# Two of four weight sums made by an accumulating transfer, in a decoder layer on one Trainium2 core

## The chip, the cores and the metric

The kernel runs on one core of a Trainium2 chip. A core has five engines with a queue each, which run side by side and wait for one another through semaphores: TensorE (PE, matrix products; its weight loads are listed as PEld), VectorE (DVE), ScalarE (ACT), GpSimd (POOL) and SyncE (SP). Transfers between the memory and the core's own store (SBUF) are issued from an engine's queue and carried out by 16 DMA engines. Matrix products go to PSUM, a small store from which ScalarE and VectorE fetch them. The metric is the device time of one execution in microseconds (us); less is better.

## The reference

One decoder layer on 512 tokens of width 1024, all in float32: a SwiGLU feed-forward (hidden width 2816), a mixing part with dilated attention (12 heads of 128) beside a gated recurrence, and a second feed-forward, each with a norm before and after. Cut to what matters here:

```python
def swiglu(x, w_gate, w_up, w_down):
    return (jax.nn.silu(x @ w_gate) * (x @ w_up)) @ w_down

f = swiglu(rms_norm(h, ffn1_norm_pre[l]), ffn1_w_gate[l], ffn1_w_up[l], ffn1_w_down[l])
h = h + 0.5 * rms_norm(f, ffn1_norm_post[l])
u = rms_norm(h, mix_norm_pre[l])
proj = u @ w_in[l]                       # q, k, v, xr, yr and the branch gates
...
f = swiglu(rms_norm(h, ffn2_norm_pre[l]), ffn2_w_gate[l], ffn2_w_up[l], ffn2_w_down[l])
h = h + 0.5 * rms_norm(f, ffn2_norm_post[l])
```

The weights that this case is about are blocks of 128 columns of the up and gate matrices of both feed-forwards, and pairs of such blocks of `w_in` (a query block with a key block, and pairs of branch-gate blocks).

## The kernel before

**Split products.** TensorE works with a reduced float format (float32r). Each float32 operand is split in a high and a low part: ScalarE copies the value into the reduced format (L302) and VectorE subtracts that from the value (L303). A product then takes three matmuls: high by high, high by low, low by high.

**Seven products for eight.** Two column blocks of 128 (u and g) times the activations are a two-by-two block product: each weight block has two halves along the contracted dimension (u0, u1, g0, g1, each 128 x 512 as stored), and the activations are halved along the contracted dimension and along the tokens. A scheme of the Strassen kind makes it with seven products, p1 to p7, of half-size operands. It needs sums of weight blocks: u0+u1, u0+g0, u0+u1+g0 and u0+u1+g0+g1. A pair of blocks that is treated so is called a pair below. There are 16 in the first feed-forward (hidden blocks 6 to 21), 12 for queries and keys and 4 for branch gates in the attention stage, and 19 in the second feed-forward (blocks 3 to 21): 51.

**`w_forms`** prepares a pair. It loads the block u = (u0, u1) and the block g = (g0, g1), 512 KB each, into two tiles `raw` (tag raw, four buffers, filled through SyncE's queue), makes the four sums on VectorE (L691, L692, L693, L696; the first two go to a tile `s12` of tag `s`, two buffers), and splits all into four tiles: a (g0 for p1, g1 for p2), b (the tile s12, for p6 and p5), c (u after its first half was overwritten, for p7 and p4), and d (for p3). a, b and c come from the four buffers of tag w8, d from the two of tag w4. The products run in the order p1, p5, p6, p2, p7, p3, p4 (`seven_on`, `seven_wide`), only in the feed-forward blocks below 5 in the order p1, p2, p6, p5, p7, p4, p3 (`seven`). Their results are moved and summed out of PSUM by ScalarE and VectorE (L743, L792, L800, L950, L955).

**Order.** Tags are pools of buffers: a tile waits until an earlier holder of its buffer has been read for the last time. The order of the instructions in each engine's queue is laid out beforehand by a planner that takes the ready instruction of highest priority by its own estimate of durations and landings; `high_priority` moves the weight work ahead by AHEAD = 100 places and the fetching of results from PSUM by EVAC = 200. The pair for block f+1 is prepared in front of the products of block f. At run time each queue is worked in order, and an instruction that waits holds up all behind it.

**Around it.** In the feed-forwards the down product runs in between, four steps for each part of four hidden blocks, with forms of its own in the w8 buffers (`d_forms`, L986 to L1000). The tag `s` in the same pools also holds two sums of the activations (`forms_of`, tiles ts, or `x_forms`) until these are split, before the first pairs of a stage. GpSimd's queue issues other transfers: residual rows (h, kept), gains (L449), copies of activation forms (L655) and a rearrangement of values (L1239). The recurrence stage prepares its pairs with another function, `w_forms_within`, which uses no tile of tag `s`.

Of the kernel before, what the change touches and what calls it, by code (L numbers as in the profile page):

```python
# [10 lines left out]
F32 = mybir.dt.float32  # L11
F32R = mybir.dt.float32r
AF = mybir.ActivationFunctionType
ALU = mybir.AluOpType
AX = mybir.AxisListType

P = 128
T = 512
D = 1024
KC = D // P  # L20
NF = 22
FF_PARTS = ((0, 4), (4, 8), (8, 12), (12, 16), (16, 22))
NSTD = {1: 6, 2: 3}

SEVEN = range(4)
STEPS_AT = {1: ((6, 7, 7, 8), range(9, 13), range(13, 17), range(17, 21)),
# [5 lines left out]
RAW_W = 1024  # L32
# [3 lines left out]
AHEAD = 100  # L36
# [29 lines left out]
def ffn_order(n):  # L66

    order = [("std", f) for f in range(NSTD[n])]  # L70
    after = {}
# [3 lines left out]
    ready = False  # L75
    for f in range(NSTD[n], NF):
        if not ready:
# [106 lines left out]
def hybrid_layer(ctx: ExitStack, tc: tile.TileContext, xT: bass.AP, xN: bass.AP, wst: bass.AP,  # L184
                 first: bass.AP, rows: bass.AP, consts: bass.AP, bias: bass.AP, out: bass.AP):
    nc = tc.nc
    DVE, ACT, PE = nc.vector, nc.scalar, nc.tensor
# [3 lines left out]
    wpool = ctx.enter_context(tc.tile_pool(name="wpool", bufs=4))  # L191
# [39 lines left out]
    groups = stream_groups()  # L231
    state = {"g": 0, "i": 0, "off": 0, "raw": None, "ahead": AHEAD, "split": None}
# [68 lines left out]
    def split(dh, dl, src):  # L301
        state["split"] = ACT.activation(dh, src, AF.Copy).ins  # L302
        state["low"] = DVE.tensor_sub(dl, src, dh.bitcast(F32)).ins  # L303
# [377 lines left out]

    spool = [None]

    def w_forms(key):

        with tc.high_priority(offset=AHEAD):
            ur, gr = raw_two(key)
            u0, u1, g0, g1 = (r[:, i * 512:(i + 1) * 512] for r in (ur, gr) for i in range(2))
            s12 = spool[0].tile([P, 2, 512], F32, name="s12", tag="s", bufs=2)
            s1, s2 = s12[:, 0, :], s12[:, 1, :]  # L690
            DVE.tensor_add(s2, u0, u1)  # L691
            DVE.tensor_add(s1, s2, g0)  # L692
            DVE.tensor_add(u0, u0, g0)  # L693
            a, b, c, d = w8(), w8(), w8(), w4()
            split(a[:, 0, :], a[:, 1, :], gr)
            DVE.tensor_add(g1, s1, g1)  # L696
            split(b[:, 0, :], b[:, 1, :], s12.rearrange("p s c -> p (s c)"))
            split(c[:, 0, :], c[:, 1, :], ur)
            split(d[:, 0, :], d[:, 1, :], g1)
            lo, hi = slice(0, 512), slice(512, 1024)  # L700
            return {"p1": a[:, :, lo], "p2": a[:, :, hi], "p6": b[:, :, lo], "p5": b[:, :, hi],
                    "p7": c[:, :, lo], "p4": c[:, :, hi], "p3": d}
# [156 lines left out]
    def ffn(n, x, r, forms_x, apool, pss):  # L859
# [206 lines left out]

        keys = [(w, n, i) for i in range(NSTD[n]) for w in ("gate", "up")]
        forms = {}
        for ev in ffn_order(n):
            if ev[0] == "std":  # L1070
                j = ev[1]
                while len(pss) < 2 * j + 2:
                    pss.append(acc_ps())
                    gemm(pss[-1], fetch(keys[len(pss) - 1]), x)
                with tc.high_priority(offset=EVAC if j == NSTD[n] - 1 else 0):
                    std_out(pss[2 * j], pss[2 * j + 1], j)

                for step in steps[j:] if j == min(NSTD[n], 4) - 1 else steps[j:j + 1]:
                    step()
# [44 lines left out]
    for k in range(KC):  # L1124
        wh, wl, raw = wts[k]
# [77 lines left out]
    with ExitStack() as mx:  # L1203
# [291 lines left out]
        for c in range(0, KC, 2):  # L1495
            g, u = tmp("g"), tmp("u")
# [12 lines left out]
    with ExitStack() as mx:  # L1509
# [183 lines left out]
        for c in range(KC):  # L1693
            if c < 3:
                ps = pss[c]
            else:
# [25 lines left out]
    grow5, _ = gains(ap2, 4)  # L1722
# [138 lines left out]
```

## Time and profile before

| what | value |
|---|---|
| runs | 1209.45, 1208.63, 1209.24 us, median 1209.24 |
| profiled execution | 1209.61 us, its span 1207.8 us |
| busy PE / DVE / ACT / POOL | 1198.6 / 1033.3 / 831.8 / 26.1 us |
| first feed-forward's pairs | about 72 to 310 us from the span's start |
| pairs of attention | about 407 to 665 us |
| second feed-forward's pairs | about 898 to 1150 us |
| moved by DMA | 149.77 MB |

The span runs from the first to the last instruction. In the lists, "L303 DVE TENSOR_TENSOR w<-s,w" is line 303 of the kernel on VectorE, writing a tile w from tiles s and w; "x51 | 62.2, 1220 | 3.2 <-ACT w L302" are count, busy us, mean ns of one, and the us that the engine stood idle in front of them, with what ended that. Rows in order of time have start, duration, engine, line, operation and tiles. The rows of waits have the engine and line that waited, what for, the us in total, how often and the longest. Rows of stretches have, for each engine, the busy us and the number of instructions, then the granted clock, the DMA engines' busy share and GB/s.

### The profile page before, as it was taken

The page shows a single profiled execution, that of the slowest core. Times are in us where ns is not written, and L with a number is a line of the kernel's source. Part 1 is how long each engine was busy: PE and PEld are TensorE (multiplying, and loading weights), DVE is VectorE, ACT ScalarE, POOL GpSimd, SP SyncE. Part 2 cuts the span into 40 slices and gives each one's busy share as a digit, 9 for nine tenths or more (in the row PEclk, how much of TensorE's full clock was granted, in tenths as well). Part 3 has the DMA queues.
Part 4 walks back from the last instruction along what each step waited for, and adds up shares of the span by engine and source line. Part 5 has one row for each costly group of instructions (what it writes and reads, how often), then busy time and mean ns, then how long its engine had stood idle before and what let it go on. Part 6 is the DMA issues. An engine that isn't in the chain of part 4 may idle for free.

```text
span 1207.8 us, 18850 instructions
## 1 busy us (share of the span) xinstructions
PE 1198.6 (99%) x7222; PEld 1070.1 (89%) x7222; DVE 1033.3 (86%) x1626; ACT 831.8 (69%) x1447; POOL 26.1 (2%) x51
## 2 busy tenths in 40 slices
PE   9999999999999999999999999999999999999997
PEld 8889999999888888888888888888899999999996
DVE  7999888989689899999868999774799888889964
ACT  6566787887566576777736988734566687778763
POOL 0000000000011000000000000000100000000000
PEclk9999999999999999999999999999999999999999
DMA  7224343434725232222323532235443333333441
GB/s 267 88 92 139 120 139 109 137 117 150 250 106 154 71 101 91 89 87 80 122 67 110 176 121 88 88 107 189 140 142 121 121 125 117 128 120 126 125 173 70
DMA packets 45819, 149.77 MB, mean 124 GB/s; under 512 B 5152, under 2 KB 8608, under 8 KB 45728
## 3 DMA queue, kind: packets, MB, share of 16 engines
q1 hardware_dynamic: 38160, 131.09, 32.9%
q0 software_dynamic: 7280, 17.30, 4.3%
q8 instruction: 56, 0.92, 0.3%
q14 instruction: 35, 0.29, 0.1%
q10 hardware_dynamic: 288, 0.17, 0.0%
HBM read 138.06 MB, written 6.29 MB: 120 GB/s over the span
## 4 chain that ended last, share of the span: by engine, by line
PE 92%; DVE 4%; DMA 2%; ACT 1%; issue 1%; DVEq 0%; ACTq 0%
PE acc L779 10%; PE acc L729 9%; PE acc L731 9%; PE acc L730 9%; PE acc L315 7%; PE acc L317 7%; PE acc L316 7%; PE acc L780 5%; PE aux L1043 4%; PE aux L1044 4%; PE aux L1045 4%; PE acc L433 2%; PE acc L432 2%; PE acc L431 2%; DVE w L303 2%; DMA raw<-in_w 2%
## 5 line engine op out<-in xcount | busy, mean ns | idle before, releaser
L303 DVE TENSOR_TENSOR w<-raw,w 128x1024 fp32r<-128x1024 f32 (+1 forms) x272 | 296.9, 1097 | 32.2 <-ACT w L302 31.4
L302 ACT ACTIVATE w<-raw 128x1024 fp32r<-128x1024 f32 (+1 forms) x272 | 259.5, 958 | 90.0 <-PE acc L317 48.2
L729 PE MATMUL acc<-big,w 128*128 128x256 f32 x860 | 243.6, 283 | 0.0
L731 PE MATMUL acc<-big,w 128*128 128x256 f32 x860 | 243.4, 283 | 0.0
L730 PE MATMUL acc<-big,w 128*128 128x256 f32 x860 | 243.3, 283 | 0.0
L729 PEld LDWEIGHTS acc<-big,w 128*128 128x128 f32 x860 | 164.8, 192 | 1.8
L730 PEld LDWEIGHTS acc<-big,w 128*128 128x128 f32 x860 | 164.8, 192 | 1.5
L731 PEld LDWEIGHTS acc<-big,w 128*128 128x128 f32 x860 | 164.8, 192 | 0.0
L779 PE MATMUL acc<-big,w 128*128 128x512 f32 x380 | 136.5, 398 | 0.0
L780 PE MATMUL acc<-big,w 128*128 128x256 f32 x380 | 107.5, 283 | 0.0
L1043 PE MATMUL aux<-w,xf 128*128 128x512 f32 x224 | 87.3, 392 | 0.6 <-ACT w L302 0.6
L1044 PE MATMUL aux<-w,xf 128*128 128x512 f32 x224 | 87.5, 391 | 0.0
L1045 PE MATMUL aux<-w,xf 128*128 128x512 f32 x224 | 87.2, 389 | 0.0
L779 PEld LDWEIGHTS acc<-big,w 128*128 128x128 f32 x380 | 71.4, 188 | 16.0 <-ACT acc L784 0.2
L780 PEld LDWEIGHTS acc<-big,w 128*128 128x128 f32 x380 | 71.7, 189 | 0.3
L303 DVE TENSOR_TENSOR w<-s,w 128x1024 fp32r<-128x1024 f32 x51 | 62.2, 1220 | 3.2 <-ACT w L302 2.7
L315 PE MATMUL acc<-xf,w 128*128 128x512 f32 (+1 forms) x168 | 59.2, 354 | 0.0
L316 PE MATMUL acc<-xf,w 128*128 128x512 f32 (+1 forms) x168 | 58.7, 350 | 0.0
L317 PE MATMUL acc<-xf,w 128*128 128x512 f32 (+1 forms) x168 | 58.5, 349 | 0.0
L302 ACT ACTIVATE w<-s 128x1024 fp32r<-128x1024 f32 x51 | 53.9, 1057 | 6.2 <-PE acc L731 3.0
L779 PE MATMUL acc<-rb,w 128*128 128x512 f32 x152 | 55.5, 397 | 0.0
L743 ACT ACTIVATE c<-acc 128x256 f32<-128x256 f32 x68 | 25.8, 383 | 35.3 <-PE acc L731 35.3
(458 smaller groups left out, 2919.5 us busy)
## 6 DMA issues: line engine op xcount, KB each, us to landing
raw<-in_w SPq DMA_DIRECT2D x232, 512.0 KB, 3.5
big<-xf POOLq DMA_DIRECT2D x6, 512.0 KB, 3.3
gains<-in_rows POOLq DMA_DIRECT2D x5, 512.0 KB, 5.4
h<-in_x SPq DMA_DIRECT2D x8, 256.0 KB, 5.1
h<-in_xn POOLq DMA_DIRECT2D x4, 512.0 KB, 6.7
kept_m<-h POOLq DMA_DIRECT2D x4, 512.0 KB, 2.9
vals<-in_w SPq DMA_DIRECT2D x4, 512.0 KB, 6.0
h<-kept_m POOLq DMA_DIRECT2D x4, 512.0 KB, 6.2
```

Source lines behind the costliest of these rows:

```text
L302: state["split"] = ACT.activation(dh, src, AF.Copy).ins
L303: state["low"] = DVE.tensor_sub(dl, src, dh.bitcast(F32)).ins
L315: PE.matmul(ps, wh, xh, start=first, stop=False)
L316: PE.matmul(ps, wh, xl, start=False, stop=False)
L317: PE.matmul(ps, wl, xh, start=False, stop=last)
L729: PE.matmul(ps, wh, xh, start=start and k == 0, stop=False, skip_group_check=True)
L730: PE.matmul(ps, wh, xl, start=False, stop=False, skip_group_check=True)
L731: PE.matmul(ps, wl, xh, start=False, stop=k == 3, skip_group_check=True)
L779: PE.matmul(part, wh, at(BOTH, k), start=start and k == 0, stop=False, skip_group_check=True)
L780: PE.matmul(cross, wl, at(0, k), start=False, stop=k == 3, skip_group_check=True)
L1043: PE.matmul(ps, xh, wh, start=first and j == 0, stop=False, skip_group_check=True)
L1044: PE.matmul(ps, xh, wl, start=False, stop=False, skip_group_check=True)
```

## The change

For every pair that `w_forms` prepares, u0+u1 and u0+g0 no longer come from VectorE. GpSimd's queue issues a transfer that puts u0 twice into the tile of tag `s`, and then a second one that adds u1 to the first half and g0 to the second half as it writes. g is loaded as before, now as the first of SyncE's two loads of the pair; of u only u1 is loaded, into the second half of its tile, and the first half takes u0+u1+g0, which VectorE makes from the sum and g0. VectorE also still makes the sum of all four. Tile b now serves p5 and p7, and tile c serves p6 and p4.

```diff
+def SUMMED(key):
+    return True
...
+    def raw_sums(key):
+
+        (g, i), off = (state["g"], state["i"]), state["off"]
...
+        def at(o, *dims):
+            return bass.AP(tensor=wst.tensor, offset=wst.offset + off + o, ap=[[RAW_W, P], *dims, [1, T]])
+
+        s = spool[0].tile([P, 2, T], F32, name="s12", tag="s", bufs=2)
+        nc.gpsimd.dma_start(s, at(0, [0, 2]))
+        nc.gpsimd.dma_start(s, at(T, [P * RAW_W - T, 2]), accum_op=ALU.add)
+        gr, ur = (wpool.tile([P, RAW_W], F32, name="raw", tag="raw", bufs=4) for _ in range(2))
+        nc.sync.dma_start(gr, bass.AP(tensor=wst.tensor, offset=wst.offset + off + P * RAW_W,
+                                      ap=[[RAW_W, P], [1, RAW_W]]))
+        nc.sync.dma_start(ur[:, T:], at(T))
+        state["g"], state["off"] = g + 2, off + 2 * P * RAW_W
+        return s, ur, gr
+
+    def w_forms_summed(key):
+
+        with tc.high_priority(offset=AHEAD):
+            s, ur, gr = raw_sums(key)
+            a, b, c, d = w8(), w8(), w8(), w4()
+            split(a[:, 0, :], a[:, 1, :], gr)
+            DVE.tensor_add(ur[:, :T], s[:, 0, :], gr[:, :T])
+            split(b[:, 0, :], b[:, 1, :], s.rearrange("p s c -> p (s c)"))
+            split(c[:, 0, :], c[:, 1, :], ur)
+            DVE.tensor_add(gr[:, T:], ur[:, :T], gr[:, T:])
+            split(d[:, 0, :], d[:, 1, :], gr[:, T:])
+            lo, hi = slice(0, T), slice(T, D)
+            return {"p1": a[:, :, lo], "p2": a[:, :, hi], "p5": b[:, :, lo], "p7": b[:, :, hi],
+                    "p6": c[:, :, lo], "p4": c[:, :, hi], "p3": d}
+
     def w_forms(key):
 
+        if SUMMED(key):
+            return w_forms_summed(key)
         with tc.high_priority(offset=AHEAD):
             ur, gr = raw_two(key)
```

More of the change, by code (lines that the diff above doesn't have):

```diff
@@ L682, in hybrid_layer @@
     spool = [None]
+    def raw_sums(key):
+        (g, i), off = (state["g"], state["i"]), state["off"]
+        assert i == 0 and groups[g] == [(key + ("lo",), 0, RAW_W)] and groups[g + 1] == [(key + ("hi",), 0, RAW_W)]
+        def at(o, *dims):
[22 more added lines that the diff above has]
+                    "p6": c[:, :, lo], "p4": c[:, :, hi], "p3": d}
     def w_forms(key):
+        if SUMMED(key):
+            return w_forms_summed(key)
         with tc.high_priority(offset=AHEAD):
```

## The prediction

> **What bounds the kernel now.** I read the page first: the span, the engines' busy time and the chain that ended last.
>
> ```profile
> span 1207.8 us, 18850 instructions
> PE 1198.6 (99%) x7222; PEld 1070.1 (89%) x7222; DVE 1033.3 (86%) x1626; ACT 831.8 (69%) x1447; POOL 26.1 (2%) x51
> PEclk9999999999999999999999999999999999999999
> DMA packets 45819, 149.77 MB, mean 124 GB/s; under 512 B 5152, under 2 KB 8608, under 8 KB 45728
> PE 92%; DVE 4%; DMA 2%; ACT 1%; issue 1%; DVEq 0%; ACTq 0%
> ```
>
> TensorE is busy for 1198.6 of 1207.8 us and carries 92% of the chain; the clock is granted whole. VectorE, which the change relieves, carries 4%. Since a busy PE is not PE at its peak, I next looked at how matmuls follow one another in order of time, here where the first pair of the second feed-forward begins:
>
> ```profile
> 898.10 0.39 PE L316 MATMUL acc<-xf,w 128*128 128x512 f32 x1
> 898.32 0.39 PE L317 MATMUL acc<-xf,w 128*128 128x512 f32 x1
> 898.55 0.28 PE L729 MATMUL acc<-big,w 128*128 128x256 f32 x1
> 898.66 0.28 PE L730 MATMUL acc<-big,w 128*128 128x256 f32 x1
> 898.78 0.28 PE L731 MATMUL acc<-big,w 128*128 128x256 f32 x1
> ```
>
> A 512-wide matmul starts 0.22 us after the one before it, a 256-wide one 0.12 us, so one product of 12 narrow matmuls takes 1.44 us and a pair of seven 10.1 us. What could still be taken away is what TensorE waits for: the list of waits by engine, first TensorE's own and then its weight loads', and the stretches by stage (us; PE, PEld, DVE, ACT, POOL busy).
>
> ```profile
> PE aux L1120 <- DVE eps L228: 1.1, 1, 1.1
> PE aux L1378 <- DVE qk L792: 0.7, 1, 0.7
> PEld aux L1378 <- DVE qk L792: 1.0, 1, 1.0
> 60.00:290.00 230.00, 230.00 (x1590) 215.38 (x1589) 207.59 (x274) 174.09 (x292) 0.00 (x0) 1.00 0.38 123
> 395.00:590.00 195.00, 194.34 (x1179) 171.33 (x1178) 184.91 (x400) 135.67 (x296) 0.00 (x0) 1.00 0.27 86
> 880.00:1150.00 270.00, 269.38 (x1914) 253.98 (x1913) 240.99 (x317) 200.13 (x332) 1.28 (x2) 1.00 0.39 123
> ```
>
> In the three stages that have the pairs, PE idles 0, 0.66 and 0.62 us. Its longest wait for VectorE inside them is 1.0 us at the first attention scores. VectorE is tightest in attention, 184.91 of 195 us. So VectorE is no bound of the span anywhere; freed time there is worth nearly nothing, and the question is what the new transfers cost.
>
> **The change part by part.** *Removed from VectorE.* Two adds a pair, the sum of u0 and u1 (L691) and that of u0 and g0 (L693); the two others stay.
>
> ```profile
> L691 DVE TENSOR_TENSOR s<-raw 128x512 f32<-128x512 f32 x51 | 34.9, 684 | 6.1 <-DMA raw<-in_w 6.0
> L693 DVE TENSOR_TENSOR raw<-raw 128x512 f32<-128x512 f32 x51 | 34.8, 682 | 0.0
> L302 ACT ACTIVATE w<-s 128x1024 fp32r<-128x1024 f32 x51 | 53.9, 1057 | 6.2 <-PE acc L731 3.0 <-PE acc L317 1.5 <-PE acc L1274 0.3
> L303 DVE TENSOR_TENSOR w<-s,w 128x1024 fp32r<-128x1024 f32 x51 | 62.2, 1220 | 3.2 <-ACT w L302 2.7
> ```
>
> That is 34.9 + 34.8 = 69.7 us of VectorE work, 1.37 us a pair. On the path it is worth between 0 and the 1.0 us wait named above plus the 1.28 us that PE idles in the two later stages, together 2.3. I take -1.
>
> *Added: traffic.* A pair moves 1 MB now. Then it is 0.5 (u0 twice), 0.5 (accumulated), 0.5 (gate) and 0.25 (u1 again), so 1.75 MB: 51 x 0.79 million bytes = 40 MB on 149.8. The mean rate goes from 124 to about 157 GB/s; the stretches above at 123 GB/s load the DMA engines 0.38 to 0.39, so there is room. Cost 0; if the room were not there, the raw loads would be late.
>
> *Added: the chain of two transfers.* No accumulating transfer is in this trace. The nearest rows are the plain ones that GpSimd issues, and SyncE's raw load (KB each, median us from issue to landing):
>
> ```profile
> raw<-in_w SPq DMA_DIRECT2D x232, 512.0 KB, 3.5
> big<-xf POOLq DMA_DIRECT2D x6, 512.0 KB, 3.3
> gains<-in_rows POOLq DMA_DIRECT2D x5, 512.0 KB, 5.4
> h<-in_xn POOLq DMA_DIRECT2D x4, 512.0 KB, 6.7
> kept_m<-h POOLq DMA_DIRECT2D x4, 512.0 KB, 2.9
> 301.82 1.05 POOL L1151 DMA_DIRECT2D h<-in_xn  x2 [8.46 <-PE acc L731]
> ```
>
> Issuing costs POOL 1.05 / 2 = 0.53 us; 102 issues are 54 us on an engine that is 2% busy. The second waits for the first to land. A leg is 2.9 to 6.7 us, so the chain from the free buffer to the sum is 5.8 at least; with the accumulating leg at twice the slowest it is 6.7 + 13.4 = 20 at most. I take 5.4 + 6 = about 11.5: the gains row is nearest, also a broadcast read from memory. [...]
>
> *Moved: when it can start.* The sums' buffer (tag s, two of them) is now filled by POOL's queue instead of VectorE, so the chain starts when the low split (L303) of the pair two earlier ends. In attention and in the first feed-forward, VectorE's rows for two pairs two apart, and the TensorE matmul that begins the later pair's second product:
>
> ```profile
> 424.70 1.23 DVE L303 TENSOR_TENSOR w<-s,w 128x1024 fp32r<-128x1024 f32 x1 [0.52 <-ACT w L302]
> 431.02 0.68 DVE L691 TENSOR_TENSOR s<-raw 128x512 f32<-128x512 f32 x1
> 434.37 0.68 DVE L692 TENSOR_TENSOR s<-s,raw 128x512 f32<-128x512 f32 x1
> 452.82 0.40 PE L779 MATMUL acc<-big,w 128*128 128x512 f32 x1
> 161.55 1.22 DVE L303 TENSOR_TENSOR w<-s,w 128x1024 fp32r<-128x1024 f32 x1
> 180.00 0.69 DVE L691 TENSOR_TENSOR s<-raw 128x512 f32<-128x512 f32 x1 [1.90 <-DMA raw<-in_w]
> 181.74 0.69 DVE L692 TENSOR_TENSOR s<-s,raw 128x512 f32<-128x512 f32 x1
> 198.02 0.28 PE L729 MATMUL acc<-big,w 128*128 128x256 f32 x1
> ```
>
> Feed-forward: buffer free at 162.8, first add at 180.0. A chain of 11.5 us lands at 174.3, ahead of the gate's raw load that the remaining add needs too. Cost 0; the cover is 198.0 - 162.8 = 35 us less about 3 for add and splits, so even 20 us is covered. Attention: free at 425.9, needed by TensorE at 452.8 less 3, so 24 us; also covered. But VectorE works in order, and today's sum adds there stand 5.1 and 8.4 us after the buffer came free. The planner orders by its own idea of a landing. If the add is put some 8.5 us behind, VectorE stands 11.5 - 8.5 = 3 us with evacuations (L792, L800) queued behind it, and TensorE waits for those. Attention's idle VectorE time is 10.1 us plus 16 x 1.37 = 22, so 32 us, and about nine early pairs x 3 = 27 us of standing just fits; only the local lateness reaches TensorE. I take 0.45 us a pair, 4 us in all; the bounds are 0 (chain of 8.5 or less) and all of the 27.
>
> *Moved: which form sits in which buffer.* Now p6 shares a split with p5, and p7 with p4; then p5 is with p7, and p6 with p4. In the order p1, p5, p6, p2, p7, p3, p4 the middle tile of w8 comes free after the fifth product instead of the third, and the last tile is needed at the third instead of the fifth. From free to needed, the last tile had seven products between (10.1 us) in back-to-back pairs and now has four (5.8). Its making is one ACT pass and one VectorE pass, 1.06 + 1.22 = 2.3 us, so 3.5 us of queueing are allowed. Cost 0 as long as that cover holds; a queue 0.5 us longer would cost 25 us over 51 pairs. I take 1.
>
> *Start of the second feed-forward.* Both buffers hold sums of the activations until their splits end.
>
> ```profile
> 880.95 1.22 DVE L303 TENSOR_TENSOR big<-ts,big 128x1024 fp32r<-128x1024 f32 x1
> 882.14 0.74 POOL L655 DMA_DIRECT2D big<-xf  x1 [2.96 <-issue]
> 899.60 1.21 DVE L303 TENSOR_TENSOR big<-ts,big 128x1024 fp32r<-128x1024 f32 x1
> 911.50 0.28 PE L729 MATMUL acc<-tx,w 128*128 128x256 f32 x1
> ```
>
> These pairs run p1, p2, p6, p5, so c is wanted third. The first pair's buffer is free at 882.2; behind POOL's copy (to 882.9) its chain runs to 894.4 and its splits end at about 898. Its third product starts two after its first, at 898.55 + 2 x 1.44 = 901.4: covered. The second pair's chain starts at 900.8, lands at 912.3, and its c form needs add and ACT split, 0.68 + 1.06, so 914; TensorE wants it at 911.5. That is 2.5 us of stall, 0 to 11 by the chain's bounds (5.8 to 20). Without the removed adds the planner may split those sums earlier, so I take 2.
>
> *Queues.* POOL's other transfers (gains, h, kept) run in order with the new ones but stand at the ends of stages, where no pair follows. SyncE has two issues a pair as before, the gate first. Cost 0.
>
> The sum is -1 + 4 + 1 + 2 = +6 us on the profiled execution's 1209.6 us, which is 0.4 above the median of 1209.24: about 1215.
>
> **The rivals.** *Hidden* (about 1209.5): the chain is 8.5 us or less, or the planner puts the add late enough. For it speaks the 24 to 35 us of cover and the saved 69.7 us; against it the 5.4 and 6.7 us legs. It decides as soon as VectorE never stands more than the few us that its queue can spare.
>
> *Slow accumulation* (about 1265): if the chain passes 24 us, TensorE waits for it in attention itself: a chain of 30 plus 3.5 for splits is 33.5 us for two pairs, 16.8 each, against about 13 now (16 pairs in 195 us, some of it scores), so 16 x 3.5 = 56 us; the feed-forward (about 15 us a pair, two 30) just loses. Against it stands that 512 KB lands in 3 to 7 us in every row. [...]
>
> *Faster* (about 1206.5), the other side: VectorE's shorter queue removes the wait at the scores and PE's idle in both later stages, the 2.3 us from above, and some tenths of gaps between matmuls that a busy PE doesn't show, 2.7 in all, with the chain hidden. It decides if the queue of VectorE before the first scores gets shorter and no add stands. TensorE's waits are too small for more.
>
> **How the numbers follow.** A measurement of this kernel tells about 0.2%, 2.4 us, from no change. Stalls at some places, my forecast: 0.54, own range 1212 to 1240 (the attention bound of 27 instead of 4, less what overlaps). Hidden: 0.27, within 0.2%. Slow accumulation: 0.13. Faster: 0.06. The first two hold 0.81, so the range is 1207.5 to 1240. Faster 0.06, within 0.27, slower 0.54 + 0.13 = 0.67.
>
> **What would show it.** Right: L691 and L693 gone, VectorE's busy time down by about 70; the accumulating issues 51 times with 6 us or so to landing; VectorE waiting for the sums' transfer in 395 to 590 and PE's idle there up by some us; a gap of TensorE near the second pair of the second feed-forward; the first feed-forward still without idle. Wrong: the remaining add (s with g0) never waiting for the transfer, so the time unchanged; a landing of 15 us and more, so gaps in every pair; or TensorE waiting for weight splits (ACT w L302, DVE w L303) with the sums long there, which would be the buffer order and not the transfers.

## The result, and the profile after

The changed kernel takes 1316.62 us (1315.99 to 1320.67, 4 runs) against 1209.35 us: a ratio of 1.0894, with an interval of 1.0871 to 1.0917. It is slower by 107 us where 6 were forecast, and far outside the range given. The page of the changed kernel, its own run at 1320.67 us:

```profile
span 1318.9 us, 18938 instructions
PE 1235.0 (94%) x7222; PEld 1092.1 (83%) x7222; DVE 977.2 (74%) x1524; ACT 835.5 (63%) x1447; POOL 125.9 (10%) x153
DMA packets 67035, 189.88 MB, mean 144 GB/s; under 512 B 6784, under 2 KB 10240, under 8 KB 66944
PE 14%; DVE 5%; DMA 4%; ACT 2%; issue 2%; POOL 0%; DVEq 0%; POOLq 0%
```

The adds are gone (1626 to 1524 instructions of VectorE) and 40 MB are added, both as forecast. VectorE's instructions add up to 67 us less, but its busy time falls by 56 us only, where about 70 were forecast, since neighbours in its queue overlap by 11 us less. Its instructions are no slower: the low split of the sums takes 1.22 us (L309) as before (L303). TensorE's busy time rises by 36 us with the same 7222 matmuls: some of them run slower. The last row can't be compared with the 92% of before: this chain could be followed back only to 958.7 us and covers 357 of the 1318.9 us, and of these TensorE has about half. The same stages in stretches (first feed-forward, attention, second feed-forward; us; PE, PEld, DVE, ACT, POOL busy, granted clock, DMA share, GB/s):

```profile
60.00:338.00 278.00, 259.14 (x1724) 239.04 (x1723) 204.67 (x260) 188.83 (x315) 32.61 (x36) 0.97 0.58 160
424.00:735.00 311.00, 280.86 (x1554) 241.47 (x1553) 225.67 (x462) 180.13 (x364) 29.30 (x30) 0.97 0.45 118
960.00:1278.00 318.00, 291.11 (x1981) 271.14 (x1980) 222.14 (x286) 205.80 (x346) 37.85 (x41) 0.96 0.59 158
```

TensorE stands idle for 18.9, 30.1 and 26.9 us in stages where it was idle for 0 to 0.7, and the granted clock is 0.96 to 0.97 instead of 1.00. The DMA engines are busy for 0.58 instead of 0.38 of the first feed-forward. What TensorE waits for, and then what VectorE waits for, in the lists of waits:

```profile
PE aux L1084 <- ACT aux L1073: 18.4, 7, 3.1
PE acc L770 <- ACT c L877: 11.7, 3, 7.5
PE acc L820 <- ACT acc L825: 8.6, 4, 3.9
PE acc L820 <- DVE qk L843: 7.7, 4, 4.2
PE aux L1465 <- DVE xch L1462: 7.3, 4, 4.8
...
DVE raw L714 <- DMA s<-in_w: 60.5, 14, 6.7
DVE raw L1036 <- DMA raw<-in_w: 52.5, 7, 8.7
```

None of TensorE's waits names a sum or a transfer. It waits for seeds, that is ScalarE's copies that give an accumulator its starting value (L1073), for copies out of PSUM (L877, L825), for evacuations, in which VectorE adds up a result of PSUM (L843), and for a small product of VectorE's in the softmax (L1462); 5.6 us more are for splits of weights (L309, L308). Those stand in the queues of ScalarE and VectorE behind two waits for transfers, the last two rows: L714, the add that needs the accumulated sum, and L1036, the sum of two plain raw loads in the down projection's third step.

In the tables below, "waits" are TensorE's: the distance between the starts of two matmuls, less the usual distance of that shape (0.227, 0.120 or 0.111 us), summed where that is over 0.3 us. For the changed kernel they are 21.0 us (first feed-forward), 33.6 (attention) and 29.7 (second feed-forward with its start), 84.3 in all, against 0.3, 1.4 and 1.1 before, 2.8 in all. TensorE's clock stands at half for 64.9 us in the changed kernel (below), which costs up to half of that, 32 us, more, an estimate. (84.3 - 2.8) + 32 = 114 covers the 111 us by which the span grew. The "way to the sums" is the time from the issue of a pair's first transfer to the landing of its last, the median over the pairs of a stage.

**How attention loses.** GpSimd's rows in order of time, two pairs apart, and VectorE's between them:

```profile
437.70 0.74 POOL L699 DMA_DIRECT2D s<-in_w  x1 [7.37 <-DVE w L309]
442.32 1.21 POOL L700 DMA_DIRECT2D s<-in_w  x1 [3.88 <-DMA s<-in_w]
...
466.29 0.75 POOL L699 DMA_DIRECT2D s<-in_w  x1 [9.22 <-DVE c L841]
```

```profile
448.45 0.69 DVE L714 TENSOR_TENSOR raw<-s,raw 128x512 f32<-128x512 f32 x1 [4.22 <-DMA s<-in_w]
449.06 0.41 DVE L833 TENSOR_TENSOR c<-acc,c 128x256 f32<-128x256 f32 x1
...
463.72 0.69 DVE L714 TENSOR_TENSOR raw<-s,raw 128x512 f32<-128x512 f32 x1 [6.22 <-DMA s<-in_w]
464.33 0.42 DVE L833 TENSOR_TENSOR qk<-acc,qk 128x256 f32<-128x256 f32 x1
464.66 1.21 DVE L309 TENSOR_TENSOR w<-s,w 128x1024 fp32r<-128x1024 f32 x1
```

The first transfer goes out at 437.70, the sum is there at 448.45, 10.7 us later, and VectorE has stood 4.22 us for it with an evacuation of the running products (L833) right behind. The same 15 us on, now 6.22 us. ScalarE takes up the first pair's sums, which landed at 448.45, only here:

```profile
457.20 1.06 ACT L308 ACTIVATE w<-s 128x1024 fp32r<-128x1024 f32 x1
```

So neither TensorE nor the split waits for the sums: in the 16 pairs of attention they lie there for 8.8 to 18.7 us before ScalarE splits them. Only the add L714, early in VectorE's order, needs them at once. What the add holds up here is, beside the evacuation, the low split of the pair before (L309 at 464.66, ready since 458.26), and with it the buffer, which comes free at 465.9, 17.4 us after the sum landed; the next transfer goes out 0.4 us later. That makes a ring of two buffers, 10.7 + 17.4 + 0.4 us for two pairs, 14.3 us a pair. The ring alone isn't the bound, though: with one transfer in place of two (e8_one, below) the next one also goes out 0.4 us behind the low split, the buffers are held 21.0 us by median, and TensorE hardly waits.

**How the feed-forwards lose.** The third down step around 225 us; the issues of SyncE and GpSimd, then VectorE's, ScalarE's and TensorE's rows:

```profile
214.79 2.68 SPq L248 DMA_DIRECT2D raw<-in_w  x2
216.53 1.20 POOL L700 DMA_DIRECT2D s<-in_w  x1 [4.29 <-DMA s<-in_w]
...
225.30 1.23 DVE L1036 TENSOR_TENSOR raw<-raw 128x1024 f32<-128x1024 f32 x1 [6.85 <-DMA raw<-in_w]
226.44 1.22 DVE L309 TENSOR_TENSOR w<-sum,w 128x1024 fp32r<-128x1024 f32 x1
227.57 0.42 DVE L996 TENSOR_TENSOR u<-acc,c 128x256 f32<-128x256 f32 x1
227.91 0.42 DVE L991 TENSOR_TENSOR g<-acc,c 128x256 f32<-128x256 f32 x1
228.36 0.42 ACT L992 ACTIVATE g<-g 128x256 f32<-128x256 f32 x1 [5.76 <-DVE g L991]
231.57 0.60 ACT L1073 ACTIVATE aux<-ea 128x512 f32<-128x512 f32 x1
232.22 0.51 PE L1084 MATMUL aux<-w,xf 128*128 128x512 f32 x1 [3.08 <-ACT aux L1073]
```

VectorE stands 6.85 us for a raw load of SyncE's queue that was issued at 217.14 (the second of the two in the first row) and landed after 8.1 us; the pair's accumulating transfer, issued at 216.53 and landed at 226.5, was under way beside it. ScalarE then stands 5.76 us behind VectorE's g, its seed of the aux accumulator comes late, and TensorE stands 3.08 us. The sum itself was in time.

### The profile page after: what moved, and what is told of

Its sections match the earlier page's. It is cut to its first block, busy times and chain, and to the rows that moved or that the text cites. A ratio compares the mean times of both kernels' runs of the same rounds, so it can differ in the third digit from the quotient of the medians.

```text
span 1318.9 us, 18938 instructions
## 1 busy us (share of the span) xinstructions
PE 1235.0 (94%) x7222; PEld 1092.1 (83%) x7222; DVE 977.2 (74%) x1524; ACT 835.5 (63%) x1447; POOL 125.9 (10%) x153
## 3 DMA queue, kind: packets, MB, share of 16 engines
q0 software_dynamic: 28496, 70.79, 22.7%
## 5 line engine op out<-in xcount | busy, mean ns | idle before, releaser
L309 DVE TENSOR_TENSOR w<-raw,w 128x1024 fp32r<-128x1024 f32 (+1 forms) x272 | 296.6, 1099 | 61.0 <-ACT w L308 59.7
L308 ACT ACTIVATE w<-raw 128x1024 fp32r<-128x1024 f32 (+1 forms) x272 | 258.6, 956 | 105.8 <-PE acc L323 44.4
L770 PE MATMUL acc<-big,w 128*128 128x256 f32 x860 | 249.4, 290 | 10.7 <-ACT c L877 10.1
L771 PE MATMUL acc<-big,w 128*128 128x256 f32 x860 | 248.6, 289 | 0.0
L772 PE MATMUL acc<-big,w 128*128 128x256 f32 x860 | 248.0, 288 | 0.0
L770 PEld LDWEIGHTS acc<-big,w 128*128 128x128 f32 x860 | 170.8, 199 | 13.4 <-ACT c L877 10.5
L771 PEld LDWEIGHTS acc<-big,w 128*128 128x128 f32 x860 | 170.5, 198 | 2.1
L772 PEld LDWEIGHTS acc<-big,w 128*128 128x128 f32 x860 | 170.2, 198 | 0.0
L820 PE MATMUL acc<-big,w 128*128 128x512 f32 x380 | 142.4, 411 | 15.3 <-DVE qk L843 7.7
L1084 PE MATMUL aux<-w,xf 128*128 128x512 f32 x224 | 90.2, 408 | 23.3 <-ACT aux L1073 18.4
L821 PE MATMUL acc<-big,w 128*128 128x256 f32 x380 | 110.0, 289 | 0.0
L820 PEld LDWEIGHTS acc<-big,w 128*128 128x128 f32 x380 | 74.0, 195 | 33.9 <-issue 7.5
L1085 PE MATMUL aux<-w,xf 128*128 128x512 f32 x224 | 90.6, 404 | 3.7 <-DVE w L309 3.7
L714 DVE TENSOR_TENSOR raw<-s,raw 128x512 f32<-128x512 f32 x51 | 35.1, 687 | 74.9 <-DMA s<-in_w 60.5
L1086 PE MATMUL aux<-w,xf 128*128 128x512 f32 x224 | 90.3, 403 | 0.0
L699 POOL DMA_DIRECT2D s<-in_w x51 | 38.2, 750 | 516.1 <-DVE w L309 298.9
L700 POOL DMA_DIRECT2D s<-in_w x51 | 61.6, 1208 | 212.9 <-DMA s<-in_w 212.9
L821 PEld LDWEIGHTS acc<-big,w 128*128 128x128 f32 x380 | 74.5, 196 | 0.2
L1084 PEld LDWEIGHTS aux<-w,xf 128*128 128x128 f32 x224 | 42.6, 193 | 36.1 <-ACT aux L1073 21.5
L308 ACT ACTIVATE w<-s 128x1024 fp32r<-128x1024 f32 x51 | 53.7, 1052 | 20.3 <-DMA s<-in_w 9.8
L309 DVE TENSOR_TENSOR w<-s,w 128x1024 fp32r<-128x1024 f32 x51 | 62.2, 1220 | 4.8 <-ACT w L308 4.6
```

The costliest lines, as they stand in the source:

```text
L699: nc.gpsimd.dma_start(s, at(0, [0, 2]))
L700: nc.gpsimd.dma_start(s, at(T, [P * RAW_W - T, 2]), accum_op=ALU.add)
L770: PE.matmul(ps, wh, xh, start=start and k == 0, stop=False, skip_group_check=True)
L771: PE.matmul(ps, wh, xl, start=False, stop=False, skip_group_check=True)
L772: PE.matmul(ps, wl, xh, start=False, stop=k == 3, skip_group_check=True)
L820: PE.matmul(part, wh, at(BOTH, k), start=start and k == 0, stop=False, skip_group_check=True)
```

## The experiments

**Which part of the change.** First the order of the forms and their buffers alone, with all four sums on VectorE:

```diff
-            DVE.tensor_add(s2, u0, u1)
-            DVE.tensor_add(s1, s2, g0)
-            DVE.tensor_add(u0, u0, g0)
+            DVE.tensor_add(s1, u0, u1)
+            DVE.tensor_add(s2, u0, g0)
...
-            DVE.tensor_add(g1, s1, g1)
+            DVE.tensor_add(u0, s1, g0)
...
+            DVE.tensor_add(g1, u0, g1)
...
-            return {..., "p6": b[:, :, lo], "p5": b[:, :, hi], "p7": c[:, :, lo], "p4": c[:, :, hi], ...}
+            return {..., "p5": b[:, :, lo], "p7": b[:, :, hi], "p6": c[:, :, lo], "p4": c[:, :, hi], ...}
```

> All four sums are again made by VectorE from the two plain loads of before; only the order in which the forms are made and the halves they share are those of the change (the pair of sums u0+u1 and u0+g0 in one buffer, u0+u1+g0 beside u1 in another). If the order of the forms and the rotation of their buffers carry a part of the loss (T4), this kernel loses some 20 to 60 us of the 107. If they carry nothing, as the prediction's 1 us for them says, it stands within 2 us of the kernel before (1207 to 1211.5), and the loss belongs to the transfers.

Measured: 1218.12 us, ratio 1.0068 (1.0052 to 1.0085). Between the two expectations: a real loss of 8.6 us that the prediction put at 1, and no more than a twelfth of the whole. In its list of waits VectorE stands at the down step's sum more than before (0.9 us there), which already shows the weak place:

```profile
DVE raw L995 <- DMA raw<-in_w: 11.6, 5, 3.1
```

Then the change in the feed-forwards alone, and in attention alone:

```diff
 def SUMMED(key):
-    return True
+    return key[0] == "gu"        # second kernel: key[0] != "gu"
```

> The change in the two feed-forwards alone; attention's pairs have the kernel before's four sums on VectorE. The stages of the changed kernel are longer by about 28 us (first feed-forward), 41 us (attention) and 39 us (second feed-forward, start included). If each stage's loss is its own (the theory of contention: the accumulating transfers delay the raw loads of the same blocks), this gives 1209 + 28 + 39 = about 1276 us, and attention runs at its old length of about 270 us. If the loss comes mostly from attention's waits and spreads from there, it stands at 1225 or below.

> The change in attention alone. Theory of the chain (T1: VectorE stands at the first add until the sums have landed, and what is queued behind it is late for TensorE): 1209 + 41 = about 1250 us, with VectorE's waits at the first add as in the changed kernel (some 60 us) and the feed-forwards at their old lengths. If attention is only hurt by what the first feed-forward leaves behind, under 1220 us.

Measured: 1273.38 us (ratio 1.0528, 1.0507 to 1.0549) and 1254.92 us (1.0375, 1.0351 to 1.0399). The losses are 63.8 and 45.4 us, 109 in sum against 107: each stage loses for itself. In the second kernel the first feed-forward runs without idle, and attention's waits are 39.3 us:

```profile
60.00:310.00 250.00, 250.00 (x1736) 234.44 (x1735) 222.54 (x293) 188.11 (x316) 3.30 (x6) 1.00 0.41 133
```

**The accumulation against the transfers.** The second transfer made plain, so that it overwrites where the change adds, and two of the four sums are left out:

```diff
-        nc.gpsimd.dma_start(s, at(T, [P * RAW_W - T, 2]), accum_op=ALU.add)
+        nc.gpsimd.dma_start(s, at(T, [P * RAW_W - T, 2]))
```

> The changed kernel with its second transfer plain: it overwrites the two halves instead of adding to them, so two of the four weight sums are left out. Same bytes from the weights, same two transfers one after the other, same waits. If the accumulation itself is what is dear (its landing takes 7.7 us in the middle against 4.3 of the plain one, and raw loads beside it land after 8 us instead of 3.4), the second transfer lands after about 4.3 us, the raw loads after 3.4, and the time falls to 1215 to 1240. If it is the chain of two transfers and the additional bytes whatever their kind, it stays above 1290.

Measured: 1264.62 us (1.0455, 1.0434 to 1.0476), between the two expectations. The order of the instructions is the changed kernel's on every engine. So the accumulation costs 52 us and two plain transfers in its place still 55. From the DMA view of this kernel and of the changed one, the waits of VectorE and the queue that holds GpSimd's transfers (packets, MB, share of 16 engines):

```profile
DVE raw L1036 <- DMA raw<-in_w: 41.9, 7, 7.5
DVE raw L714 <- DMA s<-in_w: 29.7, 13, 4.8
q0 software_dynamic: 21968, 70.79, 17.3%
```

```profile
q0 software_dynamic: 28496, 70.79, 22.7%
```

17.3% of the span of 1262.7 us are 218 us, 22.7% of 1318.9 are 299: for the same bytes the 51 accumulating transfers hold the 16 engines 81 us longer, 1.6 us each. The kernel before had 4.3% of 1207.8, so 52 us, in this queue; (218 - 52) / 102 = 1.6 us is a plain transfer. An accumulating transfer thus occupies the engines twice as long as a plain one, 1.6 + 1.6 = 3.2 us against 1.6. It also has more packets: (28496 - 21968) / 51 = 128 on top of the plain one's 144.

**The transfers beside the kernel before.** In the feed-forwards alone, the change's two transfers into the buffer of the sums, which VectorE then overwrites with its own:

```diff
+            if key[0] == "gu":
+                nc.gpsimd.dma_start(s12, at(0, 0))
+                nc.gpsimd.dma_start(s12, at(T, P * RAW_W - T), accum_op=ALU.add)
             ur, gr = raw_two(key)
```

> The kernel before with its four sums on VectorE and its raw loads, and beside them, in the feed-forwards alone, the change's two transfers from the same places of the weights into the buffer of the two sums, which VectorE then overwrites. So nothing of the change's saving, its loads' order or its forms is here; only the transfers and their waits. Contention theory (T2: the accumulating transfers make the raw loads beside them land after 8 us instead of 3.4 and so delay the down projection): the loads of the down projection are late at its sum, and the kernel loses 40 us or more of the 64 that the change lost with the feed-forwards alone. Theory of the loads' order and the buffers held longer (T3): under 1220 us, beside what VectorE waits for the landing at its first add (named in the trace).

Measured: 1271.13 us (1.0511, 1.048 to 1.0541): 61.7 us, the feed-forwards' whole loss, with none of the change's order or loads. But it does not part contention from the length of the way, since VectorE also waits for the transfers' end before it may overwrite the buffer:

```profile
DVE s L697 <- DMA s<-in_w: 36.2, 9, 7.5
raw<-in_w SPq DMA_DIRECT2D x232, 512.0 KB, 4.2
```

The raw loads take 4.2 us to land instead of 3.5.

**Length against occupation.** The next five kernels part these. First one plain transfer in place of two, then one, two or three small accumulating transfers behind it, which lengthen the way with hardly any bytes; then a full second one that lengthens nothing, since it goes from the buffer to a tensor in memory and no engine's work waits for its end. In all five, two of the four sums are left out.

```diff
-        nc.gpsimd.dma_start(s, at(0, [0, 2]))
-        nc.gpsimd.dma_start(s, at(T, [P * RAW_W - T, 2]), accum_op=ALU.add)
+        nc.gpsimd.dma_start(s, at(T, [P * RAW_W - T, 2]))
+        for _ in range(3):                                   # f1_chain; 2 in f4_chain2, 1 in f5_chain1
+            nc.gpsimd.dma_start(s[:, :, :16], ..., accum_op=ALU.add)
+        nc.gpsimd.dma_start(ballast, s, accum_op=ALU.add)    # f2_traffic, in place of the loop
```

> The changed kernel without its first transfer: the second one, plain, fills the two halves alone (u1 and g0 stand where the sums should, so two of the four sums are left out). One step of 4 to 5 us instead of two of 12 or more in sum. Theory of the chain (T1): the waits at the first add go, attention stands within some us of its old length, and the kernel at 1210 to 1225. If the order of the loads and the buffers held are what costs (T3), the down projection's wait at its sum of two raw loads (42 us in the variant with two plain transfers) stays above 25 us and the time above 1235.

> One plain transfer and one accumulating one of 16 columns: a way of about 8 us (estimated 4.3 + 3.8), as the variant with two plain transfers had in attention (8.8, 1264.6 us in all). If the loss rises in proportion to the chain over the 4.0 to 4.5 us of one transfer, about 1221.6 + 83 x 4/12 = 1249; if there is a room of some us that the chain may use at no cost, under 1230.

> One plain transfer and two accumulating ones of 16 columns behind it, in place of three (the sums are left out and 16 columns of each half get wrong sums added). With three the way from the first issue to the last landing was 15.3 to 17.7 us (medians of the stages), longer than the change's 11.0 to 13.6; with two it should be about 12, the change's own, at less than half of its extra bytes. If the chain alone makes the change's loss in attention, PE's waits there stand at about 30 us as in the changed kernel (33.2). For the feed-forwards the chain's part is what this kernel loses there: the changed kernel's waits are 21.0 and 29.7 us, the variant with traffic and no chain had 14.3 and 12.7. If the two add up, some 8 to 17 us here in each and about 1265 in all; if the chain alone does it, 20 to 30 in each and about 1300.

> The variant with one plain transfer (1221.6 us; two of the four sums left out), followed into the same buffer by three accumulating transfers of 16 columns each, one after the other (the first 16 columns of each half get wrong sums added). The bytes grow by 5% of the changed kernel's second transfer, but the sums are ready only after four transfers in a row, an estimated 4.3 + 3 x 2.5 or more, about the 12 us of the change's chain. If the length of the chain is what costs (T1), the time rises to 1290 or more, near the changed kernel's 1316. If the bytes and the engines' occupation are what cost (T2), it stays below 1240.

> The variant with one plain transfer (two of the four sums left out), and behind each of these a second accumulating transfer of the same 512 KB that goes from the buffer into a scratch tensor in device memory and for whose end no engine's arithmetic waits. It puts the occupation of the change's second transfer beside the loads at the same moments, without lengthening the way to the sums. By T2 the raw loads land late again and the time rises to 1270 or more; by T1 it stays at 1220 to 1235. Between, each has its part.

| kernel | us | ratio and interval | way to the sums, first ff / attention / second ff | waits, same stages |
|---|---|---|---|---|
| one transfer (e8_one) | 1221.63 | 1.0101 (1.0072 to 1.0131) | 4.5 / 4.0 / 4.0 | 2.4 / 5.0 / 3.8 |
| and one small (f5_chain1) | 1235.05 | 1.0211 (1.0181 to 1.0240) | 8.7 / 7.4 / 9.4 | 7.2 / 6.7 / 7.9 |
| and two small (f4_chain2) | 1258.38 | 1.0404 (1.0348 to 1.0459) | 12.1 / 10.6 / 12.7 | 5.3 / 14.4 / 19.1 |
| and three small (f1_chain) | 1304.68 | 1.0787 (1.0747 to 1.0827) | 16.0 / 15.3 / 17.7 | 21.3 / 30.2 / 22.5 |
| one, and a full one aside (f2_traffic) | 1253.63 | 1.0365 (1.0335 to 1.0395) | 4.5 / 4.0 / 4.1 | 14.6 / 4.1 / 16.0 |
| the change | 1316.62 | 1.0894 (1.0871 to 1.0917) | 13.2 / 11.0 / 13.6 | 21.0 / 33.6 / 29.7 |

One transfer brings the time within 4 us of the kernel with the new order of forms alone. So the order of SyncE's loads is nearly free, and VectorE's relief brings nothing. With the way the time rises, and more steeply beyond 9 us: by 13, 23 and 46 us for about 4 us more each time. The length of the way and the occupation of the engines are each right in part, in a stage of their own. The second transfer of f2_traffic occupies as much as the change's: its queue has 24.1% of 1250.4 us, 301 us against 299. This occupation alone costs attention nothing (4.1 us of waits) and the feed-forwards 14.6 and 16.0 (12.7 without the 3.3 at the second one's start); a way as long as the change's, without its bytes, costs the first feed-forward 5.3 and attention 14.4. In the first feed-forward the two parts add up: (5.3 - 2.4) + (14.6 - 2.4) + 2.4 = 17.5 of 21.0. The lists of waits of f1_chain and of f2_traffic show the two places apart, the first at the add of the sums, the second at the down step's raw loads with the sums long there:

```profile
DVE raw L716 <- DMA s<-in_w: 78.1, 21, 12.4
```

```profile
DVE raw L1038 <- DMA raw<-in_w: 47.3, 8, 8.3
PE aux L1086 <- ACT aux L1075: 13.0, 6, 3.1
ballast<-s POOLq DMA_DIRECT2D x51, 512.0 KB, 6.3
```

A caution: the planner writes the queues anew when the number of transfers changes. Compared place by place with the change's, VectorE's order of these five kernels has another operation at 10 to 22 of the first 300 places, but at 133 to 251 of the next 800, attention among them. So the rows of the first feed-forward can be compared nearly as they stand, those of attention less strictly.

**The same order with a longer way.** Two more kernels settle attention. The first has the two plain transfers and one small accumulating one; the second is the whole change with a third transfer, which adds zeros to a column. The order of the instructions in both is the same on every engine.

```diff
         nc.gpsimd.dma_start(s, at(0, [0, 2]))
-        nc.gpsimd.dma_start(s, at(T, [P * RAW_W - T, 2]), accum_op=ALU.add)
+        nc.gpsimd.dma_start(s, at(T, [P * RAW_W - T, 2]))                     # f6_plain_chain
+        nc.gpsimd.dma_start(s[:, :, :16], ..., accum_op=ALU.add)
...
+        nc.gpsimd.dma_start(s[:, :, :1], <zeros of the constants>, accum_op=ALU.add)   # g1_zeros, behind L700
```

> The changed kernel with its second transfer plain, as in the variant with two plain transfers (1264.6 us; chain 8.8 us in attention and 10.2 to 10.9 in the feed-forwards; the sums left out), and behind it one accumulating transfer of 16 columns, which puts some 3.3 us on the chain: about 12 in attention, 13.5 in the feed-forwards, the change's own lengths at the change's own bytes, but with hardly anything accumulated. If chain and bytes make the loss together and the accumulation only through them, the time is 1305 to 1325 and TensorE's waits in attention about 30 us. If accumulating has a cost of its own beside its length, it stands at 1285 or below.

> The changed kernel, whole, with a third accumulating transfer behind its second that adds zeros to one column of each half. It puts some 3 us more on the way to the sums and some bytes more, so by length and occupation alone it is slower than the change: 1320 to 1345. But the planner reckons with one more transfer and puts the first add later in VectorE's order: in attention it stands 2 to 11 places behind the previous pair's last split of its sums in 10 of 15 pairs, where in the changed kernel it stands 1 to 22 places ahead of it in 14; the order of every engine is that of the variant of the two plain and one small transfer (1263.5). If the order written for too short a transfer is what costs in attention, TensorE's waits there fall from 33 us to 20 or less and the time to 1275 to 1305, in spite of the longer way; the feed-forwards, whose order is nearly the same, keep their 21 and 30 us of waits.

Measured: 1263.5 us (1.0444, 1.0413 to 1.0474) and 1332.35 us (1.1021, 1.1003 to 1.1040). Together with the plain variant and the change they make four fields, here with the way to the sums and the waits in attention:

| order of the queues | second transfer plain | accumulating |
|---|---|---|
| the change's | 8.8 us, waits 12.6 (1264.62) | 11.0 us, waits 33.6 (1316.62) |
| with one more transfer reckoned | 12.1 us, waits 16.0 (1263.5) | 14.4 us, waits 35.7 (1332.35) |

Both expectations of single causes fall. The longer way of f6_plain_chain costs nothing over e4_plain, so length by itself isn't it; and the later add of g1_zeros doesn't help, so the early add by itself isn't it. What holds in both rows is the difference: at the same order, 2.2 and 2.3 us more of landing bring 21 and 20 us of waits over 16 pairs, 1.3 us a pair or some 0.6 us for each us. Down a column, an order written for one more transfer bears 3.3 us more at about the same waits. So attention pays for the time by which the sums land later than the order of the queues reckons with. How long VectorE stands idle in front of the add in attention's 16 pairs shows it for all these kernels: 5.3 us (f2_traffic, 4.1 us of TensorE's waits), 5.9 (e8_one, 5.0), 13.7 (f5_chain1, 6.7), 18.5 (e4_plain, 12.6), 22.3 (f6_plain_chain, 16.0), 24.5 (f4_chain2, 14.4), 42.1 (f1_chain, 30.2), 42.5 (g1_zeros, 35.7) and 43.0 in the change (33.6). TensorE's waits are 0.5 to 0.85 of the standing, with accumulated bytes or without.

```profile
DVE raw L716 <- DMA s<-in_w: 23.8, 9, 6.3
s<-in_w POOLq DMA_DIRECT2D x51, 16.0 KB, 2.8
```

```profile
DVE raw L717 <- DMA s<-in_consts: 58.8, 17, 9.4
```

f6_plain_chain, first, has 23.8 us of standing at the add in all stages, g1_zeros 58.8, and the change had 60.5. For the first feed-forward the fields are 13.1 and 21.0, 12.1 and 25.6: there 3.2 us more of way (10.2 to 13.4) cost nothing, and the accumulation 7.9 and 13.5 us, which fits its doubled occupation.

**The clock.** Matmuls of the changed kernel run at half speed in places. The stretches around the wait at 228.75 to 232.22 us, shown above:

```profile
228.80:232.20 3.40, 0.35 (x2) 0.00 (x0) 3.40 (x6) 2.67 (x5) 0.26 (x1) 1.00 0.14 58
232.60:236.00 3.40, 3.40 (x13) 2.92 (x12) 1.69 (x2) 3.40 (x7) 0.10 (x1) 0.50 0.70 227
236.00:239.40 3.40, 3.40 (x30) 3.40 (x30) 2.10 (x3) 2.37 (x5) 1.22 (x1) 1.00 0.61 178
```

The second stretch is at clock 0.50, the third at 1.00. Two wide matmuls and two narrow ones out of the second:

```profile
233.37 0.63 PE L1084 MATMUL aux<-w,xf 128*128 128x512 f32 x1
233.79 0.63 PE L1085 MATMUL aux<-w,xf 128*128 128x512 f32 x1
```

```profile
235.07 0.41 PE L772 MATMUL acc<-big,w 128*128 128x256 f32 x1
235.29 0.41 PE L770 MATMUL acc<-big,w 128*128 128x256 f32 x1
```

They start 0.42 and 0.22 us apart, where 0.23 and 0.12 are usual. To see whether a wait alone does that, the kernel before got waits of its own: ScalarE's copy from one accumulator to the next is repeated at every fourth of the feed-forwards' pairs.

```diff
         seventh(t, w, "p1", b, True)
-        copy(b, y)
+        calls[0] += 1
+        for _ in range(14 if calls[0] % 4 == 0 else 1):      # 8 and 22 in the two others
+            copy(b, y)
```

> The kernel before, with ScalarE's copy from b to y in every fourth product of the feed-forwards' pairs (8 places) made 14 times instead of once. A copy takes 0.377 us, so TensorE waits at the third matrix of the pair for some 13 x 0.377 - 0.9 = about 4.0 us, 8 times, 32 us in all. If a wait of TensorE costs only itself, the kernel takes at most 1209 + 32 = 1241 us and the granted clock is whole elsewhere. If the clock falls to half for 3.4 us or more after a wait of over 2.5 us, as it stands behind 14 of the waits of the changed kernel, each wait costs 1.5 us or more beside itself: 1253 us or more, and 8 stretches at clock 0.5 in the trace.

> The same with 8 copies instead of one: waits of about 7 x 0.377 - 0.9 = 1.7 us at the same 8 places, 14 us in all. By the theory that waits under about 2.3 us leave the clock whole, 1209 + 14 = 1223 us and no stretch at half clock; if any wait brings it, some 12 us more.

> The kernel before with 22 copies at 8 places: the 14 copies gave waits of 2.5 to 3.4 us (with the part ahead of them) and half clock behind two of the eight, 25 us for 8 places. Eight more copies are 8 x 0.377 = 3.0 us more at each place. If each wait of over 3 us brings half clock for 3.4 us or more, the kernel is longer than with 14 copies by 8 x 3.0 = 24 us and by 6 x 1.7 = 10 us or more beside them: 1268 us or more, and 8 stretches of half clock. If the clock has nothing to do with the waits: 1258.

| copies | us | ratio and interval | waits, both feed-forwards | half clock |
|---|---|---|---|---|
| 8 (e6_gap2) | 1221.06 | 1.0097 (1.0067 to 1.0126) | 9.4 us | none |
| 14 (e5_gap4) | 1234.53 | 1.0208 (1.0174 to 1.0242) | 21.9 us | 2 stretches, 6.8 us |
| 22 (f3_gap7) | 1274.83 | 1.0540 (1.0442 to 1.0638) | 47.6 us | 9 stretches, 54.6 us |

Other matmuls stand in part of the holes (with 8 copies three of the down product, L1046 to L1048, from 132.47 to 133.33 us), so the waits were shorter than meant, and 14 copies gave half clock at only two of the eight places. With 22 copies 25.7 us more of waits cost 40 us. The profiled run with 22 copies took 1279.83 us, a loss of 70: 47.6 + 54.6 / 2 = 75 covers it; without the clock's part it would be at most 48. The other run of the same kernel had a granted clock of 0.990 instead of 0.978 and took 1269.82 us. By that clock, less the 1 to 4 us at half with which the profiled spans end, it had about 22 us at half, an estimate, and 47.6 + 11 = 59 is close to its loss of 60. The granted clock of the profiled runs with 22 and then with 8 copies:

```profile
core 0: 1278.1 us, clock 0.978
```

```profile
core 0: 1218.8 us, clock 0.999
```

No kernel here beats the one before. Its TensorE waits of over 0.3 us add up to 2.8 us behind the start, so a lighter VectorE has little more than that to gain; smaller gaps between matmuls, 15 us in all, were not traced to any engine.

## Why the prediction was wrong

Step by step, as the prediction put them:

- *Removed from VectorE, -1.* Right in kind: the adds went and nothing was gained. With one transfer and half the sums gone from VectorE the time is 1221.63, not below the 1218.12 of the order alone.
- *Added: traffic, cost 0.* Wrong, and the largest error. "There is room" was read from a mean share of 0.38. The loads that matter are a few in each part of four blocks, and they are needed at once; the share in the mean says nothing of these moments. A second transfer beside them costs 14.6 and 16.0 us of waits in the feed-forwards without lengthening anything, and the accumulating form occupies the engines twice as long as was counted, 3.2 us against 1.6. The sentence "if the room were not there, the raw loads would be late" named the mechanism and gave it no price.
- *Added: the chain of two transfers, 11.5 us.* Right: 11.0 in attention, 13.2 and 13.6 in the feed-forwards. The legs were 4.3 and 7.6 us by median against 5.4 + 6. The 6 and the bound of twice the slowest leg, 13.4, were the author's estimates, since no transfer of before accumulates. Where it is the only one (e8_one), the plain leg still takes 4.0 in attention.
- *Attention, 4.* The mechanism was right (VectorE stands at the add, evacuations behind it), the term was mis-sized tenfold: 45 us by e3_att. "24 us; also covered" holds for TensorE's own need, as the sums lay there for 8.8 us and more before their split. Two sub-steps failed. The standing itself was put at 27 us at most, in nine pairs; it was 43.0 us, in 11 of 16 pairs and up to 6.2 us at once, and as it held up the low split behind it, it also made the next transfer later. And "VectorE's idle time just fits" spent idle time that lies elsewhere: what was late behind the add was late for TensorE at once. TensorE's waits came to 33.6 us for the 43.0 of standing, 2.1 a pair where 0.45 were taken. At the same order 2.2 us of later landing cost 1.3 us a pair, half clock not counted.
- *Feed-forwards, chain cost 0.* Nearly right: a way of the change's length without its bytes gives 5.3 us of waits in the first. The stage lost by the term above.
- *Form order, 1.* Mis-sized: 8.6 us by e1_order.
- *Start of the second feed-forward, 2.* Right in kind, mis-sized: the waits there (L770 for L877) are 11.7 us, 7.5 the longest; the bound given was 11.
- *Queues, 0.* Nearly right: e8_one, with the new order of loads and GpSimd's issues, is 3.5 us above e1_order.
- *Not in the sum at all:* the clock. The prediction counted a stall as its own length; 64.9 us at half clock add up to 32.

Of the rivals, Slow accumulation came nearest in time and had the wrong place: it needed a chain of 24 us and TensorE waiting for the sums themselves, where the chain was 11.0 us and no wait names them. (Its 16 x 3.5 = 56 us should be 16 x 3.8 = 60 by its own 16.8 and 13.) Hidden fell with its condition, that VectorE never stands more than its queue can spare.

What stays open: in attention the change's 33.6 us of waits are far more than the 14.4 of a like way without the bytes (f4_chain2), when the bytes alone give 4.1. They go with the standing at the add, 43.0 against 24.5 us, and the orders of these two kernels differ, since that of f4_chain2 reckons with three transfers; that the order is all of it isn't shown. Which load of the down step is late by its issue and which by its landing was not parted either; both show in the load issued at 217.14.

## What to carry to other kernels

A kernel whose TensorE waits for next to nothing, here 2.8 us, has next to nothing to gain from a lighter VectorE, but each new wait in an in-order queue can reach TensorE, as 33.6 us did in attention, where VectorE stood 43.0: price a new transfer by the loads that fly beside it at the moment they are needed, not by the mean share (0.38 here, and yet 14.6 and 16.0 us of waits in f2_traffic), and by where the first instruction that needs it stands in an in-order queue, not only by when TensorE wants the value. Where the order of the queues is written beforehand, a landing later than that order reckons with is paid in every round, here with some 0.6 us for each us. And where TensorE fell idle for 3 us and more in these runs, 59 times, there was 1.7 us or a multiple of it to count beside the wait, an estimate: half of a stretch of 3.4 us at clock 0.50.

## What the runs showed of the hardware that was not expected

- TensorE's granted clock fell to 0.50 behind waits of some 3 us. In the traces of all seventeen kernels, all 59 waits of 3 us and more were followed by a stretch at clock 0.50 within 3.5 us, 17 of 20 between 2.5 and 3.0, 12 of 23 between 2.0 and 2.5, and 7 of 34 between 1.5 and 2.0, where a neighbouring wait may be the cause; the stretches last 3.4, 6.8, 10.2 or 13.7 us.
- An accumulating transfer of 512 KB lands after 7.6 us (median) against 5.1 for the plain one at the same place and order, holds the 16 engines 3.2 us against 1.6, and takes GpSimd 1.21 us to issue against 0.75 (L700 and L699 of the change; the 5.1 is e4_plain's).
- A small accumulating transfer of 16 KB still takes 2.8 us to land (f6_plain_chain), and of 1 KB 2.6 (g1_zeros).
- A delay moved into the kernel before at 8 places cost more than itself: 70 us in the profiled run for 48 us of waits.
